# Six entries of two hand-written order tables rearranged, and one small matmul moved a step earlier, in a two-layer fp32 decoder trunk

## The chip, the cores and the metric

The kernel runs on one core of a Trainium2 chip. The metric is the device time of one execution in microseconds (us), given as the median of several executions. A profile is one more execution, recorded instruction by instruction; its own time is given beside its span.

## The reference, cut to what matters

Two layers work on x (512 tokens by 1024 channels, fp32). A layer is a feed-forward block (ffn1), a mixer (short convolution, gated recurrence, attention), and a second feed-forward block (ffn2). The change touches the feed-forward blocks alone:

```python
def rms_norm(x, gain):
    inv = lax.rsqrt(jnp.mean(x * x, axis=-1, keepdims=True) + EPS)
    return (x * inv) * gain

def swiglu(h, w_in, w_out):              # w_in 1024 x 5632, w_out 2816 x 1024
    gate, up = jnp.split(h @ w_in, 2, axis=-1)
    return (jax.nn.silu(gate) * up) @ w_out

for l in range(DEPTH):
    x = x + 0.5 * swiglu(rms_norm(x, ffn1_norm[l]), ffn1_w_in[l], ffn1_w_out[l])
    ...
    x = x + 0.5 * swiglu(rms_norm(x, ffn2_norm[l]), ffn2_w_in[l], ffn2_w_out[l])
```

## The kernel before

Channels lie on the 128 partitions and tokens along the free axis. Every fp32 product is made of three matmuls over a high and a low part of each operand (hi·hi, hi·lo, lo·hi; lines 346, 352 and 353). The parts are made by two instructions: ScalarE (ACT) copies the fp32 data to the rounded high part, and VectorE (DVE) subtracts it to get the low part. For weights these stand at lines 334 and 335 (streamed weights), or 731 and 733 (weights of the halved products, below); both write a tile called hl, of which there are three. For the moving operand of the halved products they stand at lines 664 to 669 and write xc.

**The entry of a feed-forward block.** There are four blocks in the run: ffn1 and ffn2 of layer 0, ffn1 and ffn2 of layer 1; this text calls their beginnings entry 1 to 4. Each block computes 22 hidden tiles of 128 channels. The first few are "covered": they are computed by an ordinary stream of matmuls on the x that is not yet normalised (only scaled by the gain), in pairs of tiles, while the mean of squares is still on its way. Six tiles are covered in entry 1, four in entries 2, 3 and 4. A pair runs over the 1024 input channels in four granules of 256. When the sum of squares (line 456, a matmul with a matrix of ones, called "squares") and the reciprocal root (lines 444 to 448, on VectorE, behind three ScalarE functions; called "norm") are there, a covered tile is finished in three steps: VectorE multiplies gate and up by the reciprocal root and so empties their PSUM banks (lines 538 and 539, "clear"), ScalarE applies SiLU to the gate (line 540, recorded under line 289), and VectorE multiplies gate by up into two quarter tiles hq (lines 621 and 624, "values").

**The halved products.** The other hidden tiles, and most of the second matrix product, are computed by Strassen's scheme in Winograd's form on halves: a unit of two hidden tiles takes seven products, in the order P1, P2, P6, P5, P7, P3, P4, of 24 or so matmuls with 256 moving columns each. The moving operands are sums of four quarters of the normalised x ("x a b" makes a quarter, line 642; "+" adds one quarter to another, line 573; a bare product name such as "P5" splits that product's operand). The held operands are sums of four quarters q0 to q3 of the weights. For the first unit of an entry, q3 is added to q2 by an accumulating DMA that GpSimd (POOL) issues; then VectorE adds q0, which gives S2 ("sum", line 719). S2 is the weight of P6. Two further accumulating DMAs use its place in time: one (line 706) adds more weights from memory to q0, which may begin once S2 and P1's split have read q0, and feeds P7; the other (line 749) adds S2 to q1, which may begin once S2 is there and P2's split has read q1, and feeds P3.

After a product, its bank is read (lines 823 to 849). For P6, ScalarE copies the bank to a tile g2 (line 830); P7 goes on accumulating into the same bank, so P7's first matmul waits for that copy. In the same way P3 waits for the copy of P5's bank to u2 (line 833). P2's bank is subtracted from g1 by VectorE (line 826), after which ScalarE applies SiLU to g1. The tiles g2 and u2 of the units and the gate and up tiles of "clear" come from the same two-buffer pools, so a unit's g2 takes the buffer of the gate tile of two allocations before, and has to wait until the "values" that read that tile have run.

**What sets the order.** Each engine runs its instructions in program order. Inside an entry that order is written out by hand: `follow` (line 295) chains the instructions of VectorE, ScalarE, TensorE, GpSimd's DMAs and SyncE's DMAs in the order of the program text. The table `ENTRY` (lines 43 to 56; one table for four covered tiles, one for six) says what is done at which place. `deal(n)` (line 558) reads place n. Places 0 to 7 (0 to 11 in entry 1) are the granules of the covered pairs, and `deal` comes ahead of the granule's own split. With four covered tiles, places 8, 9 and 10 stand ahead of the splits of the first three products' weights (P1, P2, P6), and place 11 + n comes at the very end of the work around halved product n (n = 0 is P1 of the first unit): matmuls of product n, ScalarE's copy of the weights of product n + 3, the reading of product n's bank, VectorE's split of product n + 3, the planner's own steps (`run`), then `deal`. With six covered tiles the same holds with 12, 13, 14 and 15 + n. The planner `plan` (line 78) places the weight loads, accumulations, sums and second-matrix operands of all later units by due times and a load per place; the change doesn't touch it.

```python
            product(u, p, acc, p in new, p in ("P2", "P3", "P4"), n in (0, 7))
            rest = prepare(*seq[n + LEAD]) if n + LEAD < len(seq) else None
            ...
            if rest is not None:
                rest()
            ...
            run(n)
            deal(2 * covered + LEAD + n)
```

Of the kernel before, what the change touches and what calls it, by code (L numbers as in the profile page):

```python
# [13 lines left out]
AF = mybir.ActivationFunctionType  # L14
# [12 lines left out]
DEPTH = 2  # L27
# [14 lines left out]

ENTRY = {
# [5 lines left out]
    },  # L49
# [5 lines left out]
    },  # L55
}

# [124 lines left out]
class Trunk:  # L182
# [178 lines left out]
    def stream_steps(self, jobs, parts_of, act, nk, mid=None, pre=None, deal=None, keep=False):  # L361

        k = 0
        while k < nk:
            kk = min(2, nk - k)
            if callable(mid) and k == nk - 2:
                mid()
            if pre is not None:
                pre(k)
            if deal is not None:
                deal(k)  # L380
            skew = SKEW_MOVING if jobs[0][2] is not None and jobs[0][0].shape[-1] < T else 0
            rows = self.granule(parts_of(k, kk), kk, pre is None, skew, deal is not None)
            end = k + kk == nk
            order = (
                [(job, j) for job in jobs for j in range(kk)]
                if end
                else [(job, j) for j in range(kk) for job in jobs]
            )
            for n, ((acc, cols, toks, *more), j) in enumerate(order):
                if pre is not None and n == len(order) // 2:  # L390
                    pre(k, True)
                if deal is not None and n == len(order) // 2:
                    deal(k + 1)
                ah, al = act(k + j)
                hi, lo = rows[j]
                first, last = k + j == 0 and not more, end and j == kk - 1
                if toks is None:
                    self.mm3(acc, hi[:, cols], lo[:, cols], ah, al, first, last, False, keep)
                else:
                    self.mm3(acc, ah[:, toks], al[:, toks], hi[:, cols], lo[:, cols], first, last)  # L400
            k += kk
            yield
# [62 lines left out]
        return i + self.rsqrt(self.inv, bank, r, t)  # L465


    def ffn(self, w_in, w_out, next_gain, covered, begin=None, out=None):

        nc = self.nc
        tc = self.tc
        with tc.tile_pool(name=self.n("ffn"), bufs=1) as fp:
            self.tt, self.tb = "g2", 2
            if begin is not None:
                x, gain = begin
            self.hq = {}
            self.cover(fp, w_in, w_out, covered, begin)

            f0, nf = CHUNKS[-1]
            if next_gain is not None:
                self.begin_norm(next_gain)
            last = out is not None
            self.ntog += 1
            if last:
                xs = self.turn_x()
            for dg in range(2):
                banks = self.next4()

                def parts(k, kk, dg=dg):
                    r = slice((f0 + k) * P, (f0 + k + kk) * P)
                    return [w_out[r, dg * 512 : (dg + 1) * 512]]

                spans = [slice(c, c + P) for c in (0, 128, 256, 384)]
                self.stream(
                    [
                        (bk, slice(0, T), c) if last else (bk, c, None)
                        for bk, c in zip(banks, spans)
                    ],  # L500
                    parts, lambda k: (self.hh[k // 2][:, k % 2, :], self.hl[k // 2][:, k % 2, :]), nf,
                )
                if last:
                    for i in range(4):
                        o = self.xo[dg * 4 + i]
                        nc.vector.scalar_tensor_tensor(
                            out=o, in0=banks[i], scalar=0.5, in1=xs[dg * 4 + i],
                            op0=ALU.mult, op1=ALU.add,
                        )
                        nc.sync.dma_start(out[0, spans[i], dg * T : (dg + 1) * T], o)  # L510
                    continue
                for i in range(4):
                    j = dg * 4 + i
                    xj = self.xT[:, j, :]
                    nc.vector.scalar_tensor_tensor(
                        out=xj, in0=banks[i], scalar=0.5, in1=xj,
                        op0=ALU.mult, op1=ALU.add,
                    )
                    if next_gain is not None:
                        self.norm_part(j, fp)  # L520

    def cover(self, fp, w_in, w_out, covered, begin):

# [3 lines left out]
        if begin is not None:  # L527
            x, gain = begin
        A, V = (lambda i, e=e: self.follow(e, i) for e in "av")
        norm, tiles, values = [], [], {}  # L530
        halved = self.halved(fp, w_in, w_out, covered, lambda n: deal(n))

        def clear(t):

            gi = fp.tile([P, T], F32, tag="g2", name=self.n("gi"), bufs=2)
            ui = fp.tile([P, T], F32, tag="u2", name=self.n("ui"), bufs=2)
            pg, pu = tiles[t]
            V(nc.vector.tensor_mul(gi, pg, self.inv))
            V(nc.vector.tensor_mul(ui, pu, self.inv))
            A(self.act(gi, gi, AF.Silu))  # L540
            values[t] = gi, ui

        def value(t):
# [6 lines left out]
                ))  # L550

        def squares():
            norm.append(self.bank("pt" if self.ntog % 2 == 0 else "po"))
            i = self.sum_norm(norm[0])
            if begin is None:
                self.follow("p", i)

        def deal(n):
            for what in filter(None, ENTRY[covered].get(n, "").split(", ")):
                name, *at = what.split()  # L560
                at = [int(v) if v.isdigit() else v for v in at]
                if what == "squares":
                    squares()
                elif name == "norm":
                    for e, i in self.take_norm(norm[0], fp):
                        self.follow(e, i)
                    self.table(SILU)
                    self.signs()
                elif name == "x":
                    self.normalise(fp, *at)  # L570
                elif name == "+":
                    x, y = (self.xn[tuple(v)] for v in (at[:2], at[2:]))
                    V(nc.vector.tensor_add(x, x, y))
                elif name == "clear":
                    clear(*at)
                elif name == "values":
                    value(*at)
                elif name == "load":
                    next(halved)
                elif name == "sum":  # L580
                    self.first_sum()
                else:
                    self.operand(fp, name)

        for f in range(0, covered, 2):
            banks = self.next4()

            def parts(k, kk, f=f):
# [6 lines left out]
                [(bk, slice(c, c + P), None) for bk, c in zip(banks, (0, 256, 128, 384))],  # L595
                parts, self.xact, KD, None,
                (lambda *a: self.open_x(x, gain, fp, *a)) if opening else None,
                None if opening else (lambda k, f=f: deal(2 * f + k / 2)), begin is None or f > 2,
            )
            tiles += [banks[:2], banks[2:]]  # L600
            if opening:
# [947 lines left out]
@with_exitstack  # L1549
def trunk_kernel(  # L1550
    ctx, tc, x, ffn1_norm, ffn1_w_in, ffn1_w_out, mix_norm, w_mix_in, conv_w,
    hgrn_lb_logits, hgrn_out_gain, fox_q_gain, fox_k_gain, fox_f_bias, w_mix_out,
    ffn2_norm, ffn2_w_in, ffn2_w_out, out,
):
    k = Trunk(ctx, tc)
    k.table(LNEXP)
    for l in range(DEPTH):
        k.ffn(
            ffn1_w_in[l], ffn1_w_out[l], mix_norm[l], 4 if l else 6,
            begin=(x, ffn1_norm[0]) if l == 0 else None,  # L1560
        )
        k.mix(
            l, w_mix_in[l], w_mix_out[l], conv_w[l], hgrn_out_gain[l], fox_q_gain[l],
            fox_k_gain[l], fox_f_bias[l], ffn2_norm[l], hgrn_lb_logits,
        )
        k.ffn(
            ffn2_w_in[l], ffn2_w_out[l], ffn1_norm[l + 1] if l + 1 < DEPTH else None, 4,
            out=out if l + 1 == DEPTH else None,
        )

# [28 lines left out]
```

## Time and profile before

| what | us |
|---|---|
| median of three runs | 1859.01 |
| lowest and highest of them | 1856.6, 1865.98 |
| the profiled execution: its own time | 1866.33 |
| its span, first to last instruction | 1864.2 |
| TensorE matmul busy in the span | 1838.4 (99%) |
| VectorE busy | 1478.2 (79%) |
| ScalarE busy | 1007.2 (54%) |
| GpSimd busy | 182.6 (10%) |

The mean granted TensorE clock of the profiled execution is 0.999 of full speed. The first halved product starts at 81.2, 645.7, 974.6 and 1571.9 us of the span in entries 1 to 4. A row of the timeline gives the start, the duration, the engine, the source line, the operation, and what it writes and reads; the brackets behind it give how long the engine sat idle before it and what ended that wait. A row of the waits view names the engine that waited, the tile and line that waited for another, and then the total in us, the number of times and the longest. An engine's records may overlap a little, since its instructions are pipelined: the distance between two starts is what an instruction costs its queue.

### The profile page before, as it was taken

Reading aid. Unit: us, or ns where it says so; the run is one execution under the profiler, and the core shown is the slowest. Engines: PE = TensorE matmul, PEld = TensorE weight load, DVE = VectorE, ACT = ScalarE, POOL = GpSimd, SP = SyncE. Lnnn points to the kernel's source line nnn. Section 1 sums busy time; section 2 is a strip of 40 time slices with the busy share of each in tenths; the row PEclk is TensorE's granted clock in tenths of the full one; section 3 lists DMA queues with packets and bytes.
Section 4 is the critical chain, followed back from the end, with each engine's and each line's share of the span. In section 5 each row is a group of like instructions: output and inputs, shape, how many; then the busy total and the mean of one; then the engine's idle time right before and its main releaser. Section 6 shows DMA issues by size and latency. Waiting matters only on the chain.

```text
span 1864.2 us, 33381 instructions
## 1 busy us (share of the span) xinstructions
PE 1838.4 (99%) x13532; PEld 1709.5 (92%) x13532; DVE 1478.2 (79%) x2101; ACT 1007.2 (54%) x1462; POOL 182.6 (10%) x186
## 2 busy tenths in 40 slices
PE   8999999999999999999999999999999999999999
PEld 6899999899878899999889999998998788999997
DVE  7888786677887888888678887866868878887883
ACT  4455555564666565555445555555546665555552
POOL 0011120100000101111010111201000001021210
PEclk9999999999999999999999999999999999999999
DMA  7658793232323767868275787822323238577662
GB/s 203 181 131 187 182 178 87 70 94 67 79 81 99 218 142 161 197 152 159 91 207 126 164 182 182 159 67 76 92 67 87 76 103 230 141 156 202 144 140 90
DMA packets 247529, 254.00 MB, mean 136 GB/s; under 512 B 19632, under 2 KB 232112, under 8 KB 247376
## 3 DMA queue, kind: packets, MB, share of 16 engines
q1 hardware_dynamic: 191664, 183.69, 33.0%
q0 software_dynamic: 55712, 68.18, 22.9%
q8 instruction: 106, 1.74, 0.4%
q14 instruction: 47, 0.39, 0.1%
HBM read 226.08 MB, written 2.10 MB: 122 GB/s over the span
## 4 chain that ended last, share of the span: by engine, by line
PE 85%; DVE 6%; ACT 4%; DMA 3%; issue 2%; SPq 0%; ACTq 0%; POOLq 0%; DVEq 0%
PE mm L346 13%; PE mm L353 12%; PE mm L352 12%; PE sc L346 6%; PE sc L353 6%; PE sc L352 6%; PE pt L346 5%; PE pt L352 5%; PE pt L353 5%; PE po L346 3%; PE po L352 3%; PE po L353 3%; DMA w<-in_ffn_w_in_dram 1%; DVE hl L335 1%; PE po L1448 1%
## 5 line engine op out<-in xcount | busy, mean ns | idle before, releaser
L731 ACT CAST hl<-w 128x1024 fp32r<-128x1024 f32 x322 | 337.5, 1049 | 335.2 <-PE mm L353 79.8
L733 DVE TENSOR_TENSOR hl<-w,hl 128x1024 fp32r<-128x1024 f32 x322 | 392.8, 1221 | 98.3 <-ACT hl L731 97.8
L335 DVE TENSOR_TENSOR hl<-st,hl 128x512 fp32r<-128x512 f32 (+2 forms) x196 | 166.4, 851 | 116.3 <-ACT hl L334 115.3
L334 ACT CAST hl<-st 128x512 fp32r<-128x512 f32 (+2 forms) x196 | 146.5, 750 | 194.0 <-PE mm L353 67.4
L346 PE MATMUL mm<-xc,hl 128*128 128x256 f32 (+1 forms) x730 | 203.8, 280 | 3.3 <-ACT g L830 2.8
L352 PE MATMUL mm<-xc,hl 128*128 128x256 f32 x728 | 203.5, 280 | 0.0
L353 PE MATMUL mm<-xc,hl 128*128 128x256 f32 x728 | 203.5, 279 | 0.0
L346 PE MATMUL sc<-xc,hl 128*128 128x256 f32 (+1 forms) x530 | 146.5, 277 | 3.5 <-ACT g L830 2.5
L353 PE MATMUL sc<-xc,hl 128*128 128x256 f32 x528 | 146.2, 277 | 0.0
L352 PE MATMUL sc<-xc,hl 128*128 128x256 f32 x528 | 146.0, 277 | 0.0
L346 PEld LDWEIGHTS mm<-xc,hl 128*128 128x128 f32 x730 | 137.8, 189 | 4.0 <-ACT g L830 3.1
L353 PEld LDWEIGHTS mm<-xc,hl 128*128 128x128 f32 x728 | 138.8, 191 | 0.0
L352 PEld LDWEIGHTS mm<-xc,hl 128*128 128x128 f32 x728 | 137.4, 189 | 0.0
L346 PE MATMUL pt<-xc,hl 128*128 128x256 f32 (+1 forms) x482 | 132.9, 276 | 0.3 <-ACT g L830 0.3
L352 PE MATMUL pt<-xc,hl 128*128 128x256 f32 x480 | 132.7, 277 | 0.0
L353 PE MATMUL pt<-xc,hl 128*128 128x256 f32 x480 | 132.6, 276 | 0.0
L346 PE MATMUL mm<-hl,x 128*128 128x256 f32 (+1 forms) x384 | 112.5, 293 | 0.7 <-DVE qk L1375 0.3
L346 PE MATMUL mm<-x,hl 128*128 128x512 f32 x272 | 109.7, 403 | 0.0
L353 PE MATMUL mm<-hl,x 128*128 128x256 f32 (+1 forms) x384 | 107.6, 280 | 0.0
L352 PE MATMUL mm<-hl,x 128*128 128x256 f32 (+1 forms) x384 | 107.3, 280 | 0.0
L353 PE MATMUL mm<-x,hl 128*128 128x512 f32 x272 | 106.5, 392 | 0.0
L352 PE MATMUL mm<-x,hl 128*128 128x512 f32 x272 | 106.0, 390 | 0.0
(470 smaller groups left out, 5687.2 us busy)
## 6 DMA issues: line engine op xcount, KB each, us to landing
w<-in_ffn_w_in_dram SPq DMA_DIRECT2D x140, 512.0 KB, 6.2
w<-in_ffn_w_out_dram SPq DMA_DIRECT2D x64, 512.0 KB, 3.5
w<-in_ffn_w_out_dram POOLq DMA_DIRECT2D x56, 512.0 KB, 8.9
st<-in_w_mix_in_dram SPq DMA_DIRECT2D x88, 256.0 KB, 2.7
w<-in_ffn_w_in_dram POOLq DMA_DIRECT2D x39, 512.0 KB, 8.6
st<-in_ffn_w_in_dram SPq DMA_DIRECT2D x72, 256.0 KB, 3.1
w<-S POOLq DMA_DIRECT2D x35, 512.0 KB, 4.7
st<-in_ffn_w_out_dram SPq DMA_DIRECT2D x24, 512.0 KB, 4.5
```

The lines of the kernel that those rows point to most:

```text
L334: a = nc.scalar.copy(hi, src[:, c : c + w])
L335: b = nc.vector.tensor_sub(lo, src[:, c : c + w], hi)
L346: i = nc.tensor.matmul(acc[:, c], ah, bh[:, c], start=first and c.start == 0, stop=False, skip_group_check=True,)
L352: nc.tensor.matmul(acc, ah, bl, start=False, stop=False, skip_group_check=True)
L353: i = nc.tensor.matmul(acc, al, bh, start=False, stop=last, skip_group_check=True)
L731: A(nc.scalar.copy(hi, src))
L733: return lambda: V(nc.vector.tensor_sub(lo, src, hi))
L1448: nc.tensor.matmul(self.ob[:, t0 + u * P : t0 + 2 * P], V[:, j, h % 4].rearrange("p a d -> p (a d)"), part[:, j, u:, :].rearrange("p i t - ...
```

## The change

Three things change in the entries; the arithmetic is the same.

- In entries 2, 3 and 4 "sum" (S2 of the first unit) moves from place 10 to the head of place 8: in VectorE's queue it then stands ahead of the quarter x 1 1, of the operand P5, of the weights of P1 and P2, of "clear 0" and of a "+". In entry 1 it stays at place 12.
- SiLU of a covered tile becomes a word of its own ("silu"), so that clear, SiLU and values can stand at three places. In entries 2 to 4: values 0 goes from place 12 to 11, ahead of clear 1; silu 1 from 11 to 12; values 1 from 14 to 13; clear 2 from 18 to 17, silu 2 stays at 18, values 2 goes to 19; clear 3 stays at 20, silu 3 goes to 21, values 3 to 22. In entry 1: silu 0 and 1 go from 8 to 9; silu 2 to 12, values 2 to 13; silu 3 to 13, values 3 to 14; clear 4 stays at 16, silu 4 goes to 17, values 4 to 18; clear 5 stays at 18, silu 5 goes to 19, values 5 to 20.
- "squares" is no word of the table any more but an argument. It stays ahead of granule 3 in entries 2 and 4, and goes ahead of granule 2 in entry 3. Entry 1 makes it on its own, as before.

The call of `deal` in the middle of a granule, which met no place of the table, is removed.

```diff
     4: {
-        3: "squares", 5: "norm, x 0 0", 6: "x 1 0, P1", 7: "load, x 0 1, + 0 0 0 1, P2",
-        8: "x 1 1, P5", 9: "clear 0, + 0 0 1 1", 10: "sum, + 0 1 1 1, P6, P7", 11: "clear 1",
-        12: "P3, values 0", 13: "+ 0 0 1 0", 14: "P4, values 1", 18: "clear 2, values 2",
-        20: "clear 3, values 3",
+        5: "norm, x 0 0", 6: "x 1 0, P1", 7: "load, x 0 1, + 0 0 0 1, P2", 8: "sum, x 1 1, P5",
+        9: "clear 0, + 0 0 1 1", 10: "silu 0, + 0 1 1 1, P6, P7", 11: "values 0, clear 1",
+        12: "silu 1, P3", 13: "+ 0 0 1 0, values 1", 14: "P4", 17: "clear 2", 18: "silu 2",
+        19: "values 2", 20: "clear 3", 21: "silu 3", 22: "values 3",
     },
     6: {
-        7: "norm, x 0 0", 8: "x 1 0, clear 0, clear 1", 9: "x 0 1, P1, + 0 0 0 1",
+        7: "norm, x 0 0", 8: "x 1 0, clear 0, clear 1", 9: "silu 0, silu 1, x 0 1, P1, + 0 0 0 1",
         10: "load, P2, values 0, values 1, x 1 1", 11: "P5, clear 2, + 0 0 1 1",
-        12: "P6, values 2, clear 3, sum", 13: "+ 0 1 1 1, P3, values 3", 14: "P7, + 0 0 1 0",
-        15: "P4", 16: "clear 4, values 4", 18: "clear 5, values 5",
+        12: "silu 2, P6, clear 3, sum", 13: "values 2, silu 3, + 0 1 1 1, P3", 14: "P7, values 3, + 0 0 1 0",
+        15: "P4", 16: "clear 4", 17: "silu 4", 18: "values 4, clear 5", 19: "silu 5", 20: "values 5",
     },
...
-            A(self.act(gi, gi, AF.Silu))
             values[t] = gi, ui
...
         def deal(n):
+            if n == mean and begin is None:
+                squares()
...
+                elif name == "silu":
+                    gi = values[at[0]][0]
+                    A(self.act(gi, gi, AF.Silu))
...
-            ffn1_w_in[l], ffn1_w_out[l], mix_norm[l], 4 if l else 6,
+            ffn1_w_in[l], ffn1_w_out[l], mix_norm[l], 4 if l else 6, 2,
...
-            ffn2_w_in[l], ffn2_w_out[l], ffn1_norm[l + 1] if l + 1 < DEPTH else None, 4,
+            ffn2_w_in[l], ffn2_w_out[l], ffn1_norm[l + 1] if l + 1 < DEPTH else None, 4, 3,
```

More of the change, by code (lines that the diff above doesn't have):

```diff
@@ L391, in stream_steps @@
                     pre(k, True)
-                if deal is not None and n == len(order) // 2:
-                    deal(k + 1)
                 ah, al = act(k + j)
@@ L465, in take_norm, with ffn @@
         return i + self.rsqrt(self.inv, bank, r, t)
-    def ffn(self, w_in, w_out, next_gain, covered, begin=None, out=None):
+    def ffn(self, w_in, w_out, next_gain, covered, mean=None, begin=None, out=None):
         nc = self.nc
@@ L478, in ffn @@
             self.hq = {}
-            self.cover(fp, w_in, w_out, covered, begin)
+            self.cover(fp, w_in, w_out, covered, mean, begin)
             f0, nf = CHUNKS[-1]
@@ L520, in ffn, with cover @@
                         self.norm_part(j, fp)
-    def cover(self, fp, w_in, w_out, covered, begin):
+    def cover(self, fp, w_in, w_out, covered, mean, begin):
         nc = self.nc
@@ L561, in deal @@
                 at = [int(v) if v.isdigit() else v for v in at]
-                if what == "squares":
-                    squares()
-                elif name == "norm":
+                if name == "norm":
                     for e, i in self.take_norm(norm[0], fp):
@@ L597, in cover @@
                 (lambda *a: self.open_x(x, gain, fp, *a)) if opening else None,
-                None if opening else (lambda k, f=f: deal(2 * f + k / 2)), begin is None or f > 2,
+                None if opening else (lambda k, f=f: deal(2 * f + k // 2)), begin is None or f > 2,
             )
```

## The prediction

> **What bounds the kernel now.** I read the page first, then TensorE's waits in a window around each of the four entries, then the timelines of TensorE, ScalarE (ACT), VectorE (DVE) and GpSimd (POOL) around the longest waits.
>
> ```profile
> PE 1838.4 (99%) x13532; PEld 1709.5 (92%) x13532; DVE 1478.2 (79%) x2101; ACT 1007.2 (54%) x1462; POOL 182.6 (10%) x186
> ```
>
> TensorE is the bound: 99% of the span, so an edit of orders can win only where TensorE stands still. The waits of the four entries, in order (80 to 112 us, 645 to 692, 974 to 1022, 1571 to 1618):
>
> ```profile
> PE mm L346 <- ACT g L830: 0.2, 1, 0.2
> ```
> ```profile
> PE sc L346 <- ACT g L830: 1.3, 1, 1.3
> PE sc L346 <- ACT u L833: 0.5, 1, 0.5
> PE pt L346 <- ACT g L830: 0.2, 1, 0.2
> ```
> ```profile
> PE mm L346 <- ACT g L830: 2.6, 1, 2.6
> PE po L346 <- ACT g L830: 0.5, 1, 0.5
> PE mm L346 <- ACT u L833: 0.5, 1, 0.5
> ```
> ```profile
> PE sc L346 <- ACT g L830: 1.2, 1, 1.2
> PE sc L346 <- ACT u L833: 0.5, 1, 0.5
> PE pt L346 <- ACT g L830: 0.2, 1, 0.2
> ```
>
> Ten waits, all of one sort: P7 waits until ScalarE has copied P6's bank to g2 (L830), or P3 until P5's is copied to u2 (L833). The longest of each of entries 2 to 4 is P7 of the first unit; the two shorter ones are P7 and P3 of the second unit. What one costs beyond its idle time is seen at entry 2's first, in TensorE's timeline:
>
> ```profile
> 656.58 0.28 PE L353 MATMUL pt<-xc,hl 128*128 128x256 f32 x1
> 658.14 0.39 PE L346 MATMUL sc<-xc,hl 128*128 128x256 f32 x1 [1.29 <-ACT g L830]
> 658.36 0.28 PE L352 MATMUL sc<-xc,hl 128*128 128x256 f32 x1
> ```
>
> The usual distance of two starts is 0.11 us; here one is 1.56 and the next 0.22. So 1.29 idle costs 1.45 + 0.11 = 1.56: idle plus 0.27.
>
> Entry 3 has a second loss, in the granted clock behind its long wait (columns: window, length, TensorE busy and instructions, granted clock, DMA):
>
> ```profile
> 986.00:989.34 3.34, 0.97 (x8) 1.00 0.51 82
> 989.34:992.75 3.41, 3.41 (x19) 0.50 0.00 0
> ```
>
> For 3.41 us the clock is half, behind an idle time of 2.6 us: 1.7 us more. The idle times of 1.2 and 1.3 us in entries 4 and 2 are followed by no such stretch.
>
> Losses by entry: entry 1 0.2 + 0.27 = 0.5; entry 2 2.0 + 0.8 = 2.8; entry 3 3.6 + 0.8 + 1.7 = 6.1; entry 4 1.9 + 0.8 = 2.7. In all **12.1 us, 0.65%**: the ceiling of what the change can win.
>
> **The change part by part: values 0 and silu 1 against the first wait.** ScalarE's and VectorE's timelines of entry 2:
>
> ```profile
> 653.00 1.05 ACT L731 CAST hl<-w 128x1024 fp32r<-128x1024 f32 x1 [0.66 <-DMA w<-in_ffn_w_in_dram]
> 653.96 0.63 ACT L289 ACTIVATE g<-g 128x512 f32<-128x512 f32 x1
> 654.49 1.04 ACT L669 CAST xc<-xn 128x1024 fp32r<-128x1024 f32 x1
> 655.90 1.05 ACT L731 CAST hl<-w 128x1024 fp32r<-128x1024 f32 x1 [0.38 <-DMA w<-S]
> 657.49 0.60 ACT L830 ACTIVATE g<-sc 128x512 f32<-128x512 f32 x1 [0.53 <-DVE hq L621]
> ```
> ```profile
> 634.43 1.66 DVE L642 SCALAR_TENSOR_TENSOR xn<-xT,gain,inv 128x256 f32<-128x256 f32 x4
> ...
> 641.56 1.22 DVE L733 TENSOR_TENSOR hl<-w,hl 128x1024 fp32r<-128x1024 f32 x1 [0.78 <-ACT hl L731]
> ...
> 649.86 1.23 DVE L733 TENSOR_TENSOR hl<-w,hl 128x1024 fp32r<-128x1024 f32 x1 [1.31 <-ACT hl L731]
> 651.00 0.68 DVE L538 TENSOR_TENSOR gi<-pt,inv 128x512 f32<-128x512 f32 x1
> 651.60 0.68 DVE L539 TENSOR_TENSOR ui<-pt,inv 128x512 f32<-128x512 f32 x1
> 652.20 0.68 DVE L826 TENSOR_TENSOR g<-g,sc 128x512 f32<-128x512 f32 x1
> ...
> 656.70 0.42 DVE L624 TENSOR_TENSOR hq<-gi,ui 128x256 f32<-128x256 f32 x1
> ```
>
> ScalarE waits three times on its way to L830: 0.66 us for the DMA that feeds P7's weights (the row at 653.00), 0.38 for the one that feeds P3's (655.90), and 0.53 for values 0 (657.49), because g2 takes the buffer of covered tile 0's gate, and values 0 stand behind P3's operand on VectorE. The last goes: values 0 now come right behind P5's split. VectorE's new queue, by the distances between these starts: P5's split at 649.86 as before, since it waits for ScalarE, which takes the tile that product P1 frees; 1.14 later values 0, two at 0.34 (an hq row lasts 0.42 and overlaps the next; the distance is my estimate from the 0.60 of a row that lasts 0.68); clear 1, two at 0.60; so L826 starts at 649.86 + 1.14 + 0.68 + 1.20 = 652.88 and ends at 653.56, 0.7 later than now. ScalarE behind it: SiLU of g1 at 653.6, silu 1 (moved behind it) 0.53 later, P3's operand 654.65, P3's weights 655.6, L830 656.55, end 657.15. TensorE could begin P7 at 656.70, so **a wait of about 0.5 us stays, 0.6 with its restart**, where 1.56 was. What is late next is thus ScalarE's own queue, with silu 1 in it. VectorE had 1.31 us of idle time ahead of P5's split (row 649.86), which takes up what the earlier steps push down on it.
>
> **S2 two places up.** S2 costs the same 1.13 us of VectorE wherever it stands. It is moved past ten of its instructions, to where x 1 1 begins now (row 634.43); behind it wait x 1 1, P5's operand and P1's split, which end some 4 us later, at 638.4 now and 639.5 then. What it frees are the DMAs on POOL's queue:
>
> ```profile
> 622.22 1.34 POOL L706 DMA_DIRECT2D w<-in_ffn_w_in_dram  x1 [68.88 <-DMA w<-in_ffn_w_in_dram]
> 644.47 1.29 POOL L706 DMA_DIRECT2D w<-in_ffn_w_in_dram  x1 [20.91 <-DVE S L719]
> 645.24 1.43 POOL L749 DMA_DIRECT2D w<-S  x1
> ```
>
> The second row, into q0, waited for S2 alone (P1's split was done six us before); it lands just before 653.00, 8.4 us after its issue. The third, S2 into q1, lands just before 655.90, 10.6 us. In the new order the first can go when P1's split is done, some 4 us sooner, and lands at 648.5 to 651, ahead of ScalarE's place for P7's weights (about 651.5, when P2's product frees a tile). The third is bound by P2's split, which waits for TensorE (row 641.56, end 642.8), so it goes at 643.4 to 643.7 and with the same 10.6 us lands at 654.2 or sooner, 1.4 ahead of its place at 655.6. So both DMA waits go, and neither is late next by this sum. No DMA is added; the first merely runs beside SyncE's loads, and 0 to 2.2 us of the slack could go in that (the two like transfers differ by 10.6 − 8.4). The transfer of the first row, which S2 needs, was issued 12 us ahead of S2's new place, against 8.4 to 10.6 us of duration: 1.6 us of room at the worst, and 6 more before P1's split would hold up TensorE at 645.7.
>
> **Clear 2, silu 2 and values 2; clear 3, silu 3 and values 3** against the two shorter waits. ScalarE, second unit of entry 2:
>
> ```profile
> 675.66 0.63 ACT L289 ACTIVATE g<-g 128x512 f32<-128x512 f32 x1 [0.49 <-DVE g L826]
> 676.20 1.03 ACT L731 CAST hl<-w 128x1024 fp32r<-128x1024 f32 x1
> 677.14 0.58 ACT L830 ACTIVATE g<-pt 128x512 f32<-128x512 f32 x1
> 679.18 0.63 ACT L289 ACTIVATE gi<-gi 128x512 f32<-128x512 f32 x1 [1.46 <-DVE gi L538]
> ```
>
> L830 at 677.14 hangs on VectorE's L826, which stands behind clear 2 (1.2 us), a round trip to ScalarE's SiLU, and values 2 (0.7). With clear 2 a product earlier and values 2 a product later L826 comes about 1.9 us sooner, while L830 needs to be only 0.4 sooner. Likewise the next weights' copy and L833 stand behind silu 3 (row 679.18), which waits 1.46 for clear 3; silu 3 goes behind L833, which saves more than the 0.5 + 0.27 of that wait. VectorE's work is the same; the moved values have nobody waiting but their buffer's next user, a product or more away. **Both waits go**, 0.5 and 0.8 us in entries 2 and 4, 0.8 twice in entry 3. Entry 1's 0.5 goes the same way (silu 4 no longer stands between P7's SiLU and L830).
>
> **The mean of squares in entry 3.** Entry 3's queues:
>
> ```profile
> 936.32 0.69 DVE L437 TENSOR_TENSOR sqa<-sqa,sq 128x512 f32<-128x512 f32 x1
> ```
> ```profile
> 947.55 0.69 ACT L289 ACTIVATE nr<-pt,epsc 128x512 f32<-128x512 f32 x1 [5.24 <-PE pt L456]
> ```
>
> The sum is complete at 937.0; the matmul a granule (24 matmuls of 0.227, 5.4 us) sooner comes at about 941, with 4 us to spare. It costs TensorE the same at either place: 0. ScalarE's 5.24 us of waiting goes, and VectorE's quarters start up to 5.2 us sooner. None of the ten waits hangs on that directly, since the splits ahead of them wait for TensorE to free tiles; I count it 0 on its own (bounds 0 and −0.5), as a cover for S2's move.
>
> **The sum.** Entries 2, 3 and 4 keep 0.6 each, the rest of the 12.1 goes, the half clock too, as an idle time of 0.5 us is shorter than the 1.2 and 1.3 that left the clock alone: 12.1 − 1.8 = **10.3 us**. Of the profiled execution's 1866.3 us (span 1864.2, 2.1 outside it) that leaves 1856.0. That execution is 7.3 us over the median of the runs shown, which the profile can't explain; whether the median run has the half clock isn't known. With it the median becomes 1848.7, without it 1850.4. I forecast the middle, **1849.5 us** (−0.5%).
>
> The half clock is where a rule of the notes can be weighed. The Trainium skill, "TensorE: Matmul & The Clock Gate", section "What's actually happening", says that TensorE falls to half clock after an idle window of about 3.4 us, and that the window runs freely. The length of the slow stretch agrees (3.41 us), but here a pause of 2.6 us was enough. By the page such a pause would hardly close the gate and the median's gain would be the one without it, 8.6 us; by the row it is 10.3.
>
> **The rivals.**
> - *The DMA takes the place of values 0.* S2 into q1 can't start before P2's split, and it may take longer beside other transfers. If P3's weights come as late as today (655.90), L830 follows at 656.9 and the first waits shrink by only 0.6 us: entries 2 and 4 win 0.6 + 1.3 each, entry 3 0.6 + 1.6, entry 1 0.5, and the clock stays half in entry 3, whose pause would still be 2 us: 6.5 in all, 1852.5 us. For it: two of ScalarE's three waits name a DMA. Against: 1.4 us of room.
> - *No wait stays.* If VectorE reaches L826 0.5 us sooner than I add up, all 12.1 go: 1847. Against: P5's split is bound by TensorE and what follows it is counted out of rows.
> - *The change doesn't do what it says*: the waits move to neighbouring places, as ScalarE and VectorE do the same work in the same two products. 1859. Against: VectorE's idle time of 1.31 and ScalarE's three waits are slack to be used.
> - *Slower:* S2 at the head of place 8 stops VectorE's whole queue if the accumulating DMA it needs is late. It hurts TensorE once it lands over 18 us after its issue (12 + 6); with 25 us in each of entries 2 to 4, TensorE would lose 7 us three times against the 10.3 won, which gives 1859 + 11 = 1870. Against: 8.4 to 10.6 us measured for its like.
>
> **How the numbers follow.** Chances: forecast 0.55 (by itself 1846.5 to 1852.5), DMA 0.22, no wait stays 0.08, no effect 0.09, slower 0.06. A change of 0.5% (9.3 us, below 1849.7) is about what a measurement of this kernel can tell from none; half of the forecast's and all of "no wait stays" lie beyond it, 0.36; slower 0.06; the rest, 0.58, within. The range takes in the forecast, the DMA case with the medians' own spread and the full ceiling: 1846 to 1857.
>
> **What would show it.** In the changed profile L830 of the first unit waits for nothing but its queue, and P7's wait is 0.2 to 0.6 us in entries 2 to 4; the waits on L833 and the second L830 are gone; no stretch of clock 0.50 behind entry 3; POOL's L706 is released by P1's split, not by S2; entry 3's first function on the mean (nr) comes at about 942. Wrong: a P7 wait whose ScalarE row before L830 still names "DMA w<-S", a wait of P5 for clear 1's bank, or a TensorE wait on a split (L733) of P1.

## The result, and the profile after

The changed kernel takes 1847.8 us (median of 7 executions, 1847.27 to 1848.36) against 1859.01 for the kernel before (median of 7, 1856.6 to 1869.32). The medians differ by 11.2 us (0.6%). The ratio over all executions is 0.9927, 95% interval 0.9904 to 0.9949: **faster by 0.7%**, where 1849.5 us (−0.5%) was forecast and a change of under 0.5% was held the likelier side. The profiled execution takes 1847.27 us (its span 1845.3), 19.1 us less than the 1866.33 of before. That is more than the 12.1 us that the prediction had called the ceiling, so the reason can't be all in the prediction's list.

What the prediction did list came out nearly to the digit. TensorE's waits in entries 2, 3 and 4 (the changed kernel's lines have moved by one or two: L831 is L830, L834 is L833):

```profile
PE sc L346 <- ACT g L831: 0.3, 1, 0.3
```
```profile
PE mm L346 <- ACT g L831: 0.3, 1, 0.3
```
```profile
PE sc L346 <- ACT g L831: 0.3, 1, 0.3
```

These are the only waits left in the entries; entry 1 has none. Ten waits with 7.7 us of idle time have become three with 0.9. ScalarE's timeline of entry 2, from the SiLU of g1 to the copy that P7 waits for:

```profile
653.01 0.63 ACT L289 ACTIVATE g<-g 128x512 f32<-128x512 f32 x1 [1.03 <-DVE g L827]
653.55 0.62 ACT L289 ACTIVATE gi<-gi 128x512 f32<-128x512 f32 x1
654.07 1.03 ACT L670 CAST xc<-xn 128x1024 fp32r<-128x1024 f32 x1
655.01 1.04 ACT L732 CAST hl<-w 128x1024 fp32r<-128x1024 f32 x1
655.96 0.58 ACT L831 ACTIVATE g<-sc 128x512 f32<-128x512 f32 x1
```

From 653.01 to 656.54 ScalarE is never idle, and no DMA and no "values" is named any more: the copy hangs on ScalarE's own queue, silu 1 (653.55) in it, behind VectorE's L827. The first product starts 0.57 us earlier in this execution (645.11 against 645.68); 653.01 + 0.57 is 653.6, the time worked out in the prediction. The rows of entries 3 and 4 are alike. The DMAs on POOL's queue:

```profile
639.24 1.28 POOL L707 DMA_DIRECT2D w<-in_ffn_w_in_dram  x1 [16.00 <-DMA w<-in_ffn_w_in_dram]
642.70 0.88 POOL L750 DMA_DIRECT2D w<-S  x1 [2.17 <-DVE hl L734]
```

The first goes 5.2 us sooner than before, the second 2.5 us sooner (0.6 of each because the whole entry begins sooner). The second is released by P2's split, as expected. For the first the prediction named P1's split: in entry 3 the view says so (963.31, 24.39 us idle, "DVE hl L734"), in entries 2 and 4 it names a transfer; it is not S2 in any. The mean of squares of entry 3 is taken up by ScalarE without its wait of 5.24 us, and on time (942.2 by the clock of before, as entry 3 begins 3.45 us sooner now; about 942 was expected):

```profile
938.76 0.69 ACT L289 ACTIVATE nr<-pt,epsc 128x512 f32<-128x512 f32 x1
```

And there is no stretch of half clock behind entry 3 any more.

**The part that was not listed** shows in the number of matmuls that TensorE starts in a stretch in which it never waits. Three windows of 150 us in the halved products of ffn2 of layer 0, ffn1 of layer 1 and ffn2 of layer 1, first of the kernel before, then of the kernel after (columns: window, length, busy time and number of matmuls, granted clock, DMA share, GB/s; the number includes a matmul or two that reach over the edge):

```profile
700.00:850.00 150.00, 150.00 (x1326) 1.00 0.76 171
1020.00:1170.00 150.00, 150.00 (x1276) 1.00 0.74 169
1610.00:1760.00 150.00, 150.00 (x1326) 1.00 0.74 172
```
```profile
700.00:850.00 150.00, 150.00 (x1326) 1.00 0.77 171
1020.00:1170.00 150.00, 150.00 (x1326) 1.00 0.76 172
1600.00:1750.00 150.00, 150.00 (x1326) 1.00 0.75 172
```

In ffn1 of layer 1 the kernel before starts 1276 matmuls in 150 us instead of 1326, at a granted clock of 1.00 and 100% busy. By the starts themselves it is one in 0.1178 us instead of 0.1133; this distance is called the pitch below. The busy share and the waits view don't show it. Its beginning stands in TensorE's timeline of before, at the last wait of entry 3:

```profile
1012.70 0.28 PE L353 MATMUL po<-xc,hl 128*128 128x256 f32 x1
1013.49 0.39 PE L346 MATMUL mm<-xc,hl 128*128 128x256 f32 x1 [0.52 <-ACT u L833]
1013.72 0.28 PE L352 MATMUL mm<-xc,hl 128*128 128x256 f32 x1
1013.83 0.28 PE L353 MATMUL mm<-xc,hl 128*128 128x256 f32 x1
1013.95 0.28 PE L346 MATMUL mm<-xc,hl 128*128 128x256 f32 x1
1014.07 0.28 PE L352 MATMUL mm<-xc,hl 128*128 128x256 f32 x1
```

Ahead of the wait the starts lie 0.11 apart; behind it they settle at 0.118, and stay there until the halved products end at about 1237 us. 223 us at 3.8% are 8.4 us. Adding up, over the halved products of all entries, what each start lies above 0.1133 gives 10.3 us before and 1.0 after. So of the 19.1 us between the two profiled executions about 9.3 are this longer pitch, and 9.8 are left for the waits and the half clock, for which the prediction had 10.3.

The theory to be tried, then: *waits* (idle time, restart and half clock; about 10 us in every execution) *and pitch* (a wait may leave the matmuls behind it at the longer pitch, which lasts until something breaks it; 8 to 9 us a time when it lasts to the end of the halved products, in some executions). The rivals: the waits alone, with the pitch an accident of this one execution or due to DMA traffic, addresses or the clock; and, inside the waits, that one of the three edits does it all.

### The profile page after: what moved, and what is told of

It reads as the page before. It is cut to its first block, busy times and chain, and to the rows that moved or that the text cites. A ratio compares the mean times of both kernels' runs of the same rounds, so it can differ in the third digit from the quotient of the medians.

```text
span 1845.3 us, 33378 instructions
## 1 busy us (share of the span) xinstructions
PE 1826.9 (99%) x13532; PEld 1698.6 (92%) x13532; DVE 1476.5 (80%) x2101; ACT 1005.9 (55%) x1462; POOL 182.5 (10%) x186
## 4 chain that ended last, share of the span: by engine, by line
PE 91%; DVE 4%; ACT 3%; issue 1%; DMA 1%; SPq 0%; ACTq 0%; DVEq 0%
PE mm L346 13%; PE mm L353 13%; PE mm L352 13%; PE sc L346 6%; PE sc L353 6%; PE sc L352 6%; PE pt L346 6%; PE pt L352 6%; PE pt L353 6%; PE po L346 3%; PE po L352 3%; PE po L353 3%; PE po L1449 1%; DVE hl L335 1%; ACT hl L334 1%
## 5 line engine op out<-in xcount | busy, mean ns | idle before, releaser
L734 DVE TENSOR_TENSOR hl<-w,hl 128x1024 fp32r<-128x1024 f32 x322 | 392.7, 1220 | 86.5 <-ACT hl L732 86.4
L353 PE MATMUL mm<-xc,hl 128*128 128x256 f32 x728 | 201.2, 276 | 0.0
L352 PE MATMUL mm<-xc,hl 128*128 128x256 f32 x728 | 201.1, 276 | 0.0
```

The costliest lines, as they stand in the source:

```text
L352: nc.tensor.matmul(acc, ah, bl, start=False, stop=False, skip_group_check=True)
L353: i = nc.tensor.matmul(acc, al, bh, start=False, stop=last, skip_group_check=True)
L734: return lambda: V(nc.vector.tensor_sub(lo, src, hi))
```

## The experiments

Each is timed beside the kernel before on the same chip; three chips were used, one for the parts of the change, one for before_reset, first_reset, mean_back and silu1_late, one for after_noreset, after_again and silu1_late_b, so some comparisons of two changed kernels go across chips. On the second chip the kernel before itself didn't scatter evenly: of 25 executions 11 took 1856.7 to 1860.6 us, 10 took 1865.1 to 1868.7, 3 took 1874.3 to 1876.5 and 1 took 1881.2. The first three groups lie 8 us apart, about what one stretch of the longer pitch cost in the trace. Since a median then says how often a step was taken, the lowest times are compared as well. The granted clock doesn't make the steps: its mean over an execution was 1.000 in the two lowest (1856.7, 1857.4) and in the highest (1881.2).

### One part of the change alone

**S2 alone** (sum_only):

```diff
-        8: "x 1 1, P5", 9: "clear 0, + 0 0 1 1", 10: "sum, + 0 1 1 1, P6, P7", ...
+        8: "sum, x 1 1, P5", 9: "clear 0, + 0 0 1 1", 10: "+ 0 1 1 1, P6, P7", ...
```

> The kernel before with one edit: S2 of the first unit at the head of place 8 in entries 2 to 4. Waits theory (the time won is what TensorE's waits on L830 and L833 cost, no more): both DMA waits of ScalarE go, values 0 still stand behind P3's operand, so P7's first wait falls from 1.2 to 2.6 us to about 0.3 to 0.5 us in each entry and the half clock of entry 3 goes, while the waits of the second unit stay (0.2 and 0.5 us each with 0.27 of restart): about 5.5 us won. Pitch theory (a stretch of matmuls at 0.1175 us instead of 0.1133, seen in the trace of before behind the last wait of entry 3 and lasting 220 us, is worth up to 9 us more and is entered from a wait): time scatters by up to 9 us from execution to execution, as waits stay. Rival (S2 and its DMAs are not what holds P7): P7's waits as before, nothing won.

Measured: ratio 0.9975 (0.9948 to 1.0002). Of 12 executions 3 took 1851.6 to 1853.9 us, 7 took 1860.1 to 1861.8, 2 took 1869.5 and 1869.7. The interval reaches 1; the groups say more. The lowest is 5.8 us below the lowest of before on that chip (1857.4; 5.5 expected). The wait at the first unit's P7 is 0.5 us in each entry and the second unit's waits are as they were; there is no half clock. So S2's place does hold P7, and the steps stay where the second unit's waits stay. (The profiled execution is of the lowest group, and all three windows of 150 us count 1326.)

**The places alone** (places_only): the kernel after, with

```diff
-        8: "sum, x 1 1, P5", ... 10: "silu 0, + 0 1 1 1, P6, P7",
+        8: "x 1 1, P5", ... 10: "silu 0, sum, + 0 1 1 1, P6, P7",
-            ffn1_w_in[l], ffn1_w_out[l], mix_norm[l], 4 if l else 6, 2,
+            ffn1_w_in[l], ffn1_w_out[l], mix_norm[l], 4 if l else 6, 3,
```

> The kernel after, with S2 back at place 10 and the mean of squares back at granule 3 in entry 3: only clear, SiLU and values stand apart. Waits theory: ScalarE's waits for the two DMAs stay, so P7's first wait is about 0.6 us in entries 2 and 4 (from 1.3) and still about 1.9 to 2.2 in entry 3, where the half clock may stay; the six waits of the second unit and entry 1's go: 5 to 7 us won. Pitch theory: with the second unit's waits gone, the slow stretch behind entry 3's second unit doesn't appear, and the times scatter by under 2 us. Rival (S2 does nothing): as fast as the kernel after.

Measured: 1852.3 us (1851.8 to 1853.3, 6 executions), ratio 0.9918 (0.9894 to 0.9943). TensorE's waits in entry 3, and the granted clock behind:

```profile
PE mm L346 <- ACT g L831: 2.2, 1, 2.2
```
```profile
983.00:986.40 3.40, 1.21 (x11) 1.00 0.71 114
986.40:989.80 3.40, 3.40 (x19) 0.50 0.00 0
```

Entries 2 and 4 wait 0.6 and 0.7. The lowest is 5.6 us below the lowest of before (5 to 7 expected). All as the waits theory has it, half clock included; and the times lie within 1.5 us.

**Second unit's places alone** (second_only): the order of the kernel before, written with "silu" as a word, with

```diff
-        18: "clear 2, silu 2, values 2", 20: "clear 3, silu 3, values 3",
+        17: "clear 2", 18: "silu 2", 19: "values 2", 20: "clear 3", 21: "silu 3", 22: "values 3",
```

> The kernel before, with only the places of covered tiles 2 and 3 changed as in the kernel after (clear 2 at 17, values 2 at 19, silu 3 at 21, values 3 at 22). Waits theory: the six waits of the second unit go, the three first waits stay with the half clock: 4 us won. Pitch theory: the slow stretch behind the second unit of entry 3 is gone, so the times no longer scatter: all executions near 1853. Rival: the removed waits come back in the next product, nothing won.

Measured: 1854.2 us (1852.8 to 1856.7, 6 executions), ratio 0.9929 (0.9904 to 0.9954). The three first waits are 1.3, 2.8 and 1.3 us, nothing else waits in entries 2 to 4, and no execution is a step higher. Against the lowest of before 4.6 us are won, against its median 10.8: the same edit is worth more than twice as much in the median, as no execution takes a step any more.

**Second unit's places put back** (first_only): the kernel after, with that diff the other way round.

> The kernel after, with clear, SiLU and values of covered tiles 2 and 3 back in one place each (18 and 20) in entries 2 to 4, so that the second unit's six waits come back. Waits theory: 0.2 and 0.5 us of wait with 0.27 of restart each, 4.1 us more than the kernel after, 1852. Pitch theory: in addition some executions run 5 to 9 us longer, those in which the last wait of an entry is followed by matmuls at 0.1175 us. Rival (the second unit's waits are absorbed later): as the kernel after.

Measured: ratio 0.9971 (0.9947 to 0.9995). Of 12 executions 3 took 1851.3 to 1853.1 us, 5 took 1859.5 to 1861.2, 4 took 1867.8 to 1868.8. The lowest is 4.1 above the lowest of the kernel after, which ran elsewhere (4.1 expected). The profiled execution is one of the highest, and the matmul counts say why:

```profile
690.00:840.00 150.00, 150.00 (x1276) 1.00 0.73 167
1020.00:1170.00 150.00, 150.00 (x1326) 1.00 0.74 170
1610.00:1760.00 150.00, 150.00 (x1276) 1.00 0.73 167
```

Two of the three stages run at the longer pitch, 17 us together, and these two are not the one of the profiled execution of before. Here it doesn't begin at the last wait of the entry. It begins one wait earlier, at that of the second unit's P7 (0.17 us in entry 2, 0.18 in entry 4), and is still there behind the last one, P3's on u2; in entry 2:

```profile
676.66 0.28 PE L353 MATMUL sc<-xc,hl 128*128 128x256 f32 x1
677.11 0.39 PE L346 MATMUL pt<-xc,hl 128*128 128x256 f32 x1 [0.17 <-ACT g L831]
677.33 0.28 PE L352 MATMUL pt<-xc,hl 128*128 128x256 f32 x1
677.45 0.28 PE L353 MATMUL pt<-xc,hl 128*128 128x256 f32 x1
677.57 0.28 PE L346 MATMUL pt<-xc,hl 128*128 128x256 f32 x1
...
679.92 0.28 PE L353 MATMUL pt<-xc,hl 128*128 128x256 f32 x1
680.91 0.39 PE L346 MATMUL sc<-xc,hl 128*128 128x256 f32 x1 [0.71 <-ACT u L834]
681.13 0.28 PE L352 MATMUL sc<-xc,hl 128*128 128x256 f32 x1
681.25 0.28 PE L353 MATMUL sc<-xc,hl 128*128 128x256 f32 x1
681.37 0.28 PE L346 MATMUL sc<-xc,hl 128*128 128x256 f32 x1
```

A wait can also end it: in sum_only a stretch that begins at 1005.8 us, behind the wait of the second unit's P7, is gone behind the next wait (1009.0).

### Breaking the pitch without touching a wait

A halt in the first unit (products 0 to 6) is also followed by matmuls at 0.118 in some traces, but there they end at product 7 at the latest, where the kernel splits the first matmul into two of 128 columns. TensorE's timeline of entry 3 of the kernel after, around that place (in the rows left out behind the split four more distances are about 0.12):

```profile
990.79 0.28 PE L353 MATMUL mm<-xc,hl 128*128 128x256 f32 x1
990.91 0.28 PE L346 MATMUL mm<-xc,hl 128*128 128x256 f32 x1
...
991.26 0.33 PE L346 MATMUL po<-xc,hl 128*128 128x128 f32 x2
...
992.31 0.28 PE L353 MATMUL po<-xc,hl 128*128 128x256 f32 x1
992.42 0.28 PE L346 MATMUL po<-xc,hl 128*128 128x256 f32 x1
```

If the split is what ends them, the same split behind the last wait must end the steps.

**The kernel before with one more split** (before_reset), and **first_only with it** (first_reset):

```diff
-            product(u, p, acc, p in new, p in ("P2", "P3", "P4"), n in (0, 7))
+            product(u, p, acc, p in new, p in ("P2", "P3", "P4"), n in (0, 7, 13))
```

> The kernel before with nothing of the change: only the first matmul of halved product 13 (P4 of the second unit) is split into two of 128 columns, as that of products 0 and 7 is. Pitch theory (the scatter of the kernel before is the slow pitch that starts at the last wait of an entry and runs on to the end of the halved products, 220 us later, unless two half-width matmuls break it, as those of product 7 do): the executions gather near the lowest of before, 1857 to 1859, and no stretch of over 10 us at 0.1175 us is left in the halved products behind an entry's waits; the ten waits stay. Rival (the slow pitch comes from addresses, DMA traffic or the clock, not from the rhythm after a wait): scatter as before, 1857 to 1875.

Measured: 12 executions from 1856.6 to 1861.0 us, median 1859.9, none a step higher, beside 25 of the kernel before on the same chip of which 14 were one or more; ratio 0.9965 (0.9941 to 0.9990). The ten waits are all there (1.3, 0.2, 0.5; 3.3, 0.5, 0.4; 1.2, 0.2, 0.5; 0.2). The counts of the profiled execution:

```profile
700.00:850.00 150.00, 150.00 (x1326) 1.00 0.76 171
1020.00:1170.00 150.00, 150.00 (x1326) 1.00 0.76 173
1610.00:1760.00 150.00, 150.00 (x1325) 1.00 0.74 170
```

Behind the last waits of this execution the pitch was the short one anyway, so the trace doesn't show the split at work; that the executions no longer take a step does. Two stretches of 25 us near the ends of stages remain (872.6 and 1791.7 us), about 1 us each, behind the new split.

> The kernel first_only (second unit's waits left in) with the same split at product 13. Pitch theory: executions gather at 1851 to 1853, where first_only scattered over 1851 to 1869. Waits theory alone: as first_only.

Measured: 12 executions from 1851.2 to 1855.2 us, median 1853.7, where first_only, on another chip, went up to 1868.8; ratio 0.9936 (0.9910 to 0.9963). The waits are those of first_only (0.3, 0.2, 0.7 in entry 2). Its trace shows the split at work in entry 3, where the last wait is followed by the longer pitch up to the split and, four starts behind it, by the short one again:

```profile
1008.84 0.39 PE L346 MATMUL mm<-xc,hl 128*128 128x256 f32 x1 [0.51 <-ACT u L834]
1009.07 0.28 PE L352 MATMUL mm<-xc,hl 128*128 128x256 f32 x1
1009.18 0.28 PE L353 MATMUL mm<-xc,hl 128*128 128x256 f32 x1
1009.30 0.28 PE L346 MATMUL mm<-xc,hl 128*128 128x256 f32 x1
...
1011.66 0.28 PE L353 MATMUL mm<-xc,hl 128*128 128x256 f32 x1
1011.77 0.33 PE L346 MATMUL po<-xc,hl 128*128 128x128 f32 x2
1011.94 0.33 PE L352 MATMUL po<-xc,hl 128*128 128x256 f32 x1
1012.12 0.28 PE L353 MATMUL po<-xc,hl 128*128 128x256 f32 x1
1012.23 0.28 PE L346 MATMUL po<-xc,hl 128*128 128x256 f32 x1
1012.35 0.28 PE L352 MATMUL po<-xc,hl 128*128 128x256 f32 x1
```

**The kernel after without the split at product 7** (after_noreset):

```diff
-            product(u, p, acc, p in new, p in ("P2", "P3", "P4"), n in (0, 7))
+            product(u, p, acc, p in new, p in ("P2", "P3", "P4"), n == 0)
```

> The kernel after with the first matmul of product 7 left whole (only that of product 0 is split). Pitch theory (two half-width matmuls break a slow pitch, and the one at product 7 is why a first-unit wait never costs more than itself): the waits of 0.3 us at the first unit's P7, which are followed by a few matmuls at 0.1175 us, now start stretches that run to the end of the halved products, about 250 us at 0.0043 per matmul or 9 us each, so that some executions take 1856 or 1865 instead of 1848. Rival (the stretch behind a wait ends by itself, product 7 has no part in it): 1847 to 1849 as the kernel after.

Measured: 4 executions from 1846.6 to 1849.2 us and 2 at 1856.3 and 1857.1; median 1848.7, ratio 0.9908 (0.9872 to 0.9944). A step of the size of before's is back in a kernel that never showed it (13 executions of the kernel after, with after_again below, lie within 1847.3 and 1849.8). Two of six is a small number, and the profiled execution was one of the four and shows 1326 matmuls in all three windows, so that the stretch itself wasn't seen here.

Together these three speak for a rhythm that an interruption leaves behind and the split breaks: the program's transfers, its tiles and its waits are the same with and without the split, and the steps go and come with it. That speaks against waits alone, transfers or addresses as the cause of the steps.

### The mean of squares, and the wait that is left

**The mean back at granule 3** (mean_back): the kernel after with `mix_norm[l], 4 if l else 6, 3,`.

> The kernel after with the mean of squares of entry 3 back at granule 3. By the prediction's sum its place is worth 0 to 0.5 us by itself: 1847.3 to 1848.5, entry 3 waiting 0.3 us at P7 as before. Rival (the earlier mean is what makes S2 early enough in entry 3): a wait of over 1 us at P7 in entry 3, and 1.5 us or more lost.

Measured: 1848.4 us (1847.1 to 1849.5, 8 executions), with a wait of 0.3 us in each of entries 2 to 4. The kernel after took 1847.8 and 1848.8 us on other chips, so its place is worth at most about 0.6 us, as expected, and perhaps nothing. (The ratio to before, 0.9912, 0.9876 to 0.9947, is of no use for such a difference.)

**silu 1 behind P6's copy** (silu1_late, and once more beside the kernel after as after_again and silu1_late_b):

```diff
-        12: "silu 1, P3", 13: "+ 0 0 1 0, values 1", 14: "P4", ...
+        12: "P3", 13: "silu 1, + 0 0 1 0", 14: "values 1, P4", ...
```

> The kernel after with silu 1 behind P6's copy (place 13, values 1 to 14) in entries 2 to 4. If ScalarE's own queue with silu 1 in it is what holds P7 now, as the prediction has it, the copy comes 0.53 us sooner, the three last waits of 0.3 us go with their restarts, and the time falls by 1.2 to 1.8 us to about 1846. Rival (VectorE's queue or the DMA is right behind): waits of 0.1 to 0.3 us stay, and nothing is won.

Measured: 1846.7 us (1845.6 to 1847.8, 6 executions), ratio 0.9897 (0.9850 to 0.9945), and TensorE has no wait left in any entry.

> The kernel silu1_late once more, beside the kernel after on the same chip. Waits theory: no wait is left in the entries, 1.2 to 1.8 us below the kernel after. Rival: no difference beyond 0.5 us.

> The kernel after, unchanged, as a reference on the same chip: 1847 to 1849 by every theory.

Measured on one chip: 1846.3 us (1845.4 to 1847.1; ratio to before 0.9880, 0.9850 to 0.9909) against 1848.8 (1848.3 to 1849.8; 0.9894, 0.9865 to 0.9923) for the kernel after. The two ranges don't meet: this version beats the kernel after by 2.5 us, somewhat more than the 1.8 at most that the three waits cost. The profiled execution of after_again also has two stretches of the longer pitch of some 25 us near the ends of stages (870.3 to 895.1 and 1197.3 to 1222.2), about 1 us each, as several of the traces have. They begin where no wait is on record, only one start some 0.02 us late and the next 0.11. Nor does the first unit need a wait: in silu1_late_b, which has none, entry 2 runs at the longer pitch from 657.1 us, where a start comes 0.07 us late, to product 7's split at 665.5. So what starts such a short stretch need not be a wait that the waits view lists.

## Why the prediction was right or wrong

- **The waits, their size and their cause: right.** P7's wait was to shrink to about 0.5 us in entries 2 to 4 (0.2 to 0.6 in the signs given), and is 0.31. (Its 0.5 counts from 656.70, when P7 could have started; the view counts idle time from 656.86, the end of the record before, which makes the same forecast 0.3.) L831 follows its queue; the second unit's and entry 1's waits are gone; the half clock is gone; S2's DMAs go 5.2 and 2.5 us sooner (4 and 1.5 to 1.8 forecast) and none is late.
- **The sum of the waits: right.** 10.3 us forecast. The two profiled executions differ by 9.8 us without the pitch. By the lowest times, which have no step, 9.3 us are won beside each other in the first comparison (1856.6 to 1847.3), and 7.7 on the chip of after_again (1856.1 to 1848.3). The lowest executions of before whose mean granted clock is on record (1856.1, 1856.7, 1857.4) had 1.000, where the profiled one with its half clock had 0.999: for them the forecast without the half clock, 8.6, is the one to compare.
- **The mean: not contradicted**, 0 to 0.5 forecast by itself, at most about 0.6 measured.
- **The rival with the DMA**: wrong for the full change. With S2 left at place 10 something like it happens in entry 3 (2.2 us in places_only), but the transfer that ScalarE waits for there is the one into q0 (4.14 us ahead of P7's weights, at 980.78), not S2 into q1.
- **The step that failed is the ceiling**: "In all 12.1 us, 0.65%: the ceiling of what the change can win". It priced a wait at its idle time, 0.27 us of restart and the half clock, and so put at nothing what a wait does to the matmuls behind it. In some executions it also leaves them at the longer pitch up to the next break: 8.4 us in the profiled execution. In the prediction's own trace this stood as 1276 matmuls in 150 us, against 1326 in the two other stages, a comparison that was not made; the waits view and the busy share can't show it. In the first comparison the four executions of before without a step average 1857.6 us, 9.8 above the 1847.8 of after: that is the prediction's list. The mean of all seven is 1861.5, 13.7 above; the other 3.9 us come from the three a step higher (1864.6 to 1869.3). That these three had such a stretch is worked out from the experiments, as they were not profiled.
- **From the same hole**: the prediction said that the profile couldn't explain why its execution was 7.3 us over the median. It could: that execution had one such stretch of 8.4 us, and the median execution lies among those without a step. The forecast of 1849.5 was 1.7 us too high, for two reasons: it took half of the half clock, which is 0.85 us (with all of it, 1848.7; whether the median execution had it isn't known), and the other 0.9 is not taken apart. The change beyond 0.5%, which was given 0.36, came about because the list alone won 0.53% and the steps went with the waits.
- **The clock gate.** The Trainium skill, "TensorE: Matmul & The Clock Gate", section "What's actually happening", has the clock fall to half after at least one idle window of about 3.4 us. These runs differ on the length: 2.2 us of idle time were enough in places_only, 2.6 in the kernel before, 2.8 and 3.3 in second_only and before_reset, while 1.2 and 1.3 us never did it. They agree on the slow stretch: 3.41 us in the kernel before and 3.4 in places_only. In the 3.41 us just before each of these four falls TensorE was idle for 2.2 to 2.5 us (before, 985.89 to 989.30: busy 0.93), so the whole stretch need not be idle. The fall of 6.8 us is that of second_only, whose pause ran on for 0.6 us behind it. The half clock was there in every profiled execution in which entry 3 waited 2.2 us or more.

Left open: what the longer pitch is. The traces show that the stretches of over 200 us begin at a wait of the second unit, not at each (it is there behind three of the nine last waits of entries in the traces of before, sum_only and first_only, and in two of the three it had begun at the wait before), that shorter ones also begin at a start a little late with no wait on record, that the granted clock stays at 1.00, that it is over within a few starts of two half-width matmuls, and that it costs 0.0045 us a matmul. Next waits and late starts ended it too. No run here shows what inside TensorE falls out of step, nor why one interruption does it and its like does not.

## What to carry to other kernels

Where TensorE is the bound, price a wait not only by its idle time: count the matmuls per stretch behind it and compare stages that should be alike, in more than one execution. If executions differ by steps, look for a mode that a wait can enter, and try whether a small break in the stream (here one matmul split in two) ends it before removing the waits one by one. When a helper instruction of another tile sits in an in-order queue ahead of the copy that the matmuls wait for, put it behind that copy: here silu 1 behind P6's copy won 2.5 us that way. S2 sooner, which lets its transfers start sooner, won 5.8 us by the lowest times.

## What the runs showed of the hardware that had not been expected

- A stream of 256-column matmuls with a weight load each runs at 0.1133 us or at 0.1178 us a matmul at the same granted clock of 1.00, for over 220 us on end (1326 or 1276 in 150 us).
- The longer pitch was entered at waits of 0.2 to 0.7 us, at some and not at others, for short stretches also at starts that came 0.02 to 0.2 us late, and was over within seven starts of two matmuls of 128 columns: of the kernel before 11 of 25 executions were at the lowest level, with one such split more 12 of 12 on the same chip.
- The TensorE clock was halved for 3.4 us after 2.2 us of idling, once for 6.8 us after 2.8 (second_only, entry 3; 1.2 and 1.3 us of idling never did it):

```profile
983.50:985.30 1.80, 0.00 (x0) 0.99 0.78 124
985.30:992.10 6.80, 6.19 (x29) 0.50 0.00 0
```
